# Second buffer for the accumulator tile U2, and a transposed layout of actT, in a macaron encoder block

## The chip, the cores and the metric

The kernel runs on one core of a Trainium2 chip. The metric is the device time of one execution in microseconds (us); lower is better. The core has a matrix engine (PE, with its weight loads shown as PEld), a vector engine (DVE), an activation engine (ACT), a general engine (POOL) and a queue that issues the transfers (SP). The engines run side by side and wait for each other through semaphores; each one takes its own instructions strictly in the order of the program.

## The reference, cut to what matters

One layer on x of shape (1, 1024, 1024) in float32: a half-step FFN, attention with an output projection, and a second half-step FFN. The change touches the two FFNs and everything that reads or writes the transposed activations.

```
def _swiglu(x, w_gate, w_up, w_down):
    return (jax.nn.silu(x @ w_gate) * (x @ w_up)) @ w_down

f = _swiglu(_rmsnorm(x, ffn1_pre_g[l]), ffn1_w_gate[l], ffn1_w_up[l], ffn1_w_down[l])   # D_FF = 2816
x = x + 0.5 * _rmsnorm(f, ffn1_post_g[l])
h = _rmsnorm(x, mix_pre_g[l])
qkv = h @ w_qkv[l]
...                                     # two kinds of attention
x = x + _rmsnorm(heads @ w_out[l], mix_post_g[l])
f = _swiglu(_rmsnorm(x, ffn2_pre_g[l]), ffn2_w_gate[l], ffn2_w_up[l], ffn2_w_down[l])
x = x + 0.5 * _rmsnorm(f, ffn2_post_g[l])
```

## The kernel before

**Precision.** Every float32 operand of a matrix product is split into two parts, HI and LO. A product is three matmuls per 128 rows of contraction: HI by HI, HI by LO, LO by HI (`PASSES`).

**actT** (line 67) holds the normalised activations transposed, contraction on the partitions: 2 parts, 8 token blocks `T` of 128, 8 contraction blocks `k` of 128. It lives through the whole program. `to_actT` (line 110) fills it from PE transposes, with one copy on ACT (line 107) and one subtraction on DVE (line 108) for each four blocks. It is then read by the FFNs, by the q/k/v projection (line 567, one 128x128 block at a time as weights) and, refilled by the attention's `finish` (line 870), by the output projection (line 1002, again as weights). `spare` (line 533) uses a part of it as scratch for sums of squares.

**The FFN's gate and up products.** `D_FF` is cut into 22 blocks of 128 columns. Block 0 is computed plainly (`plain`). Blocks i = 1 to 21 are computed in steps of seven products, a Strassen-like scheme on a 2 x 2 split of the contraction and of the tokens: `ORDER` is P1, P6, P2, P7, P5, P4, P3, and `LAST` (step 21 only) has P7 ahead of P2. Each product is 12 matmuls of 128x128 weights by 128x512 moving values (line 288). The moving operand of P1, P2, P4 and P3 is a slice of actT: four token blocks of one contraction block, so four runs of 128 values that lie eight blocks apart. The moving operand of P6, P7 and P5 is one of three `tx` tiles, also four runs of 128 values, four blocks apart. P1 and P2 accumulate in one PSUM tile `pa`, P6 in `pb`, P7 and P4 in `pc`, P5 and P3 in `pd`.

**The combinations** (`gate_up`, line 395) follow each product on ACT and DVE. After P1, ACT copies `pa` into the SBUF tile U2 (line 409). After P6, DVE adds `pb` into U2 (line 411). After P4, DVE forms C21 (line 423), and after P3 it adds `pd` into U2 (line 426). `glu` (lines 445 and 446) takes SiLU of one half on ACT and multiplies on DVE; P3's `glu` reads U2 last. P2 goes on accumulating in `pa`, so its first matmul may start only when line 409 has read `pa`. U2, C21 and U3 have one buffer each, so line 409 of step i+1 may write U2 only when `glu` of P3 of step i has read it.

**The weights** of each product are combined from raw gate/up blocks on POOL (lines 212 to 225) and split in HI (ACT, line 117) and LO (POOL or DVE, line 118) into a `wgu` buffer. There are five such buffers: a split for the product four places ahead is put into the program before each product (`feed`), and has to wait until an older product has released its buffer.

**Order.** All of this is written out in Python; each engine's order is the order of the calls. On ACT one step goes: split, `glu` of P3 of the step before (line 445), line 409, split, split, `glu` of P2, split, and so on.

Of the kernel before, what the change touches and what calls it, by code (L numbers as in the profile page):

```python
# [10 lines left out]
F32 = mybir.dt.float32  # L11
FR = mybir.dt.float32r
I32 = mybir.dt.int32
AF = mybir.ActivationFunctionType
# [10 lines left out]
NT = S // 128  # L25
# [6 lines left out]
HI, LO = 0, 1  # L32
# [4 lines left out]
def tile_macaron_block(ctx, tc, x, f1_pre, f1_post, f1_g, f1_u, f1_d, mix_pre, mix_post, w_qkv,  # L37
                       qg, kg, w_out, f2_pre, f2_post, f2_g, f2_u, f2_d, rope_a, rope_b, mask, out):
    nc = tc.nc
    PE, ACT, DVE, POOL, SP = nc.tensor, nc.scalar, nc.vector, nc.gpsimd, nc.sync  # L40
# [14 lines left out]
    const = ctx.enter_context(tc.tile_pool(name="const", bufs=1))  # L55
# [8 lines left out]
    POOL.memset(eps, EPS)  # L64
    ACT.activation(stat.tile([128, 1], F32, name="ss"), eps, AF.Sqrt)
    identr = const.tile([128, 128], FR, name="identr")
    actT = const.tile([128, 2, NT, 8, 128], FR, name="actT")
    ident = f32(identr)

    def load_bcast(t, g, scale=None):  # L70
# [5 lines left out]
    MARK = {}  # L76
# [19 lines left out]
    def rms_pair(srcs, junks):  # L96
        ss = stat.tile([128, 2], F32, name="ss2")
        for n in range(2):
            MARK["act"] = ACT.activation(junks[n], srcs[n], AF.Square, accum_out=ss[:, n:n + 1]).ins
        r = rstd(ss, 2, 1.0 / D)  # L100
        return [r[:, n:n + 1] for n in range(2)]

    def turn(src, hv, lv, ps):
        p = ps.tile([128, 4, 128], F32, name="pd")
        for j in range(4):
            PE.transpose(out=p[:, j, :], in_=src[:, 128 * j:128 * j + 128], identity=ident)
        ACT.activation(hv, p, AF.Copy)  # L107
        return DVE.tensor_tensor(lv, p, f32(hv), op=OP.subtract)  # L108

    def to_actT(T, xn, ps):  # L110
        for h in range(2):
            last = turn(xn[:, 512 * h:512 * h + 512], actT[:, HI, T, 4 * h:4 * h + 4, :],
                        actT[:, LO, T, 4 * h:4 * h + 4, :], ps)
        return last

    def split(hi, lo, raw, eng=POOL):
# [3 lines left out]
    class Ffn:  # L120
# [151 lines left out]

        def rhs(self, name, hl, k):
            if name == "B11":
                return actT[:, hl, 0:4, k, :]
            if name == "B21":
                return actT[:, hl, 0:4, 4 + k, :]
            if name == "B22":
                return actT[:, hl, 4:8, 4 + k, :]
            if name in ("B12", "T4"):  # L280
                return actT[:, hl, 4:8, k, :]
            return self.T[int(name[1]) - 1][:, hl, :, k, :]

        def product(self, p, w, name, first, c0=0, c1=4):
# [36 lines left out]
        def turn_combo(self, name, y, ps):  # L321
            n = int(name[1])
            for i in range(4):
                T, d = {1: (i, 0), 2: (i + 4, 1), 3: (i + 4, 0), 4: (i, 1)}[n]
                hv, lv = [actT[:, z, 4 + i, 0:4, :] if n == 4 else self.T[n - 1][:, z, i] for z in (HI, LO)]
                turn(y[:, T, 512 * d:512 * d + 512], hv, lv, ps)

        def keep(self, j):
# [65 lines left out]

        def gate_up(self, i, prod, ps, y, psd):
            def U(name):
                return self.u.tile([128, 4, 128], F32, name=name)

            tt, add, s = DVE.tensor_tensor, OP.add, self.S
            n = (self.ORDER if i < NF - 1 else self.LAST).index(prod)  # L400
            if i == 1 and 0 < n < 5:
                self.turn_combo(("T2", "T3", "T1", "T4")[n - 1], y, psd)
            p = self.bank(i, ps, self.BANK[prod])
            first = prod in ("P1", "P6", "P7", "P5")
            name = {"P1": "B11", "P6": "T2", "P7": "T3", "P5": "T1", "P2": "B21", "P4": "T4", "P3": "B22"}[prod]
            self.product(p, self.W[i, prod], name, first)
            if prod == "P1":
                s["u2"], s["c21"] = U("U2"), U("C21")
                ACT.activation(s["u2"], p, AF.Copy)  # L409
            elif prod == "P6":  # L410
                tt(s["u2"], s["u2"], p, op=add)
            elif prod == "P7":
                s["u3"] = U("U3")
                tt(s["u3"], s["u2"], p, op=add)
            elif prod == "P5":
                s["h1"] = self.new_h(i, 1)
                tt(s["u3"], s["u3"], p, op=add)  # L417
                self.glu(s["h1"][64:128], s["u3"], s["c21"])
            elif prod == "P2":
                s["h0"] = self.new_h(i, 0)  # L420
                self.glu(s["h0"][0:64], p, s["h0"])
            elif prod == "P4":
                tt(s["c21"], s["u2"], p, op=add)
                self.glu(s["h0"][64:128], s["c21"], s["h0"])
            elif prod == "P3":
                tt(s["u2"], s["u2"], p, op=add)
                self.glu(s["h1"][0:64], s["u2"], s["c21"])
            if i == NF - 1 and n == 3:
                self.close_tx(2)
                self.raw.release()  # L430
                self.load_left(self.AHEAD)
                self.open_down()
            if n == 6 and i % 2 == 1 and i < NF - 1:
                self.keep(i // 2)
            if n == 6 and i >= NF - 2:
                for half in range(2):
                    SP.dma_start(self.hd["h", i, half], self.H[i][half])
            if n == 6 and i == NF - 1:
                self.close_tx(1)
                self.u.release()  # L440
                self.us = open_pool("us" + self.tag, side=self.near)
                self.U = self.us.tile([128, 4, 512], F32, name="U")
# [67 lines left out]
    for T in range(NT):  # L510
        if T == 2:
            f1.split_plain()
        xn = y[:, T, :]
# [6 lines left out]
        last = to_actT(T, xn, psd)  # L520
# [10 lines left out]


    def spare(n):
        return actT[:, n % 2, n // 2].rearrange("p k f -> p (k f)")

    def post_norm(Ts, g, res, dst, junk, xr):
        yt = [y[:, T, :] for T in Ts]
# [8 lines left out]
    WQ = {}  # L546
# [15 lines left out]
    def qkv_mm(j, T, ps, bufs=3):  # L562
        p = ps.tile([128, 256], F32, name="pq", bufs=bufs)
        n = 0
        for k in range(8):
            for a, b in PASSES:
                PE.matmul(p, actT[:, a, T, k, :], WQ[j][:, b, k, :], start=(n == 0), stop=(n == 23))  # L567
                n += 1
        return p

# [37 lines left out]
    for t in range(2, NT + L1):  # L608
# [6 lines left out]
        if t in (2, 4):  # L615
            j = t // 2 - 1
# [7 lines left out]
        if 0 <= t - L0 < NT:  # L624
            T = TS[t - L0]
            to_actT(T, y[:, T, :], psd)
        if 0 <= t - L1 < NT:
            T = TS[t - L1]
# [166 lines left out]
    for j in range(2, 9):  # L795
# [6 lines left out]
        if 2 <= j <= 4:  # L802
            ra = tmp.tile([128, NT, 256], F32, name="ra")
            nh = 2 if j == 2 else 4
            ss = tmp.tile([128, NT, nh], F32, name="ssA")
        for T in range(NT):
            p = qkv_mm(j, T, psq)
# [62 lines left out]
    def finish(o, head, Ts, tt=None):  # L870
        b0 = 64 * (head % 2)
        t1, t2 = tt or (at.tile([64, 256], F32, name="ot1"), at.tile([128, 256], F32, name="ot2"))
        ACT.activation(t1, o[64:128, :], AF.Copy)
        ACT.activation(t2[0:64], o[0:64, :], AF.Copy)
        POOL.tensor_tensor(t2[b0:b0 + 64], t2[0:64], t1, op=OP.add)
        tv = t2[b0:b0 + 64].rearrange("p (t f) -> p t f", t=2)
        hv = actT[b0:b0 + 64, HI, Ts, head // 2, :]
        lv = actT[b0:b0 + 64, LO, Ts, head // 2, :]
        POOL.tensor_scalar(hv, tv, 1.0, 1.0, op0=OP.mult, op1=OP.mult)
        POOL.tensor_tensor(lv, tv, f32(hv), op=OP.subtract)  # L880

# [45 lines left out]
    for i in range(N + 3):  # L927
        if i < N:
            head, T, e = UN[i]
# [4 lines left out]
        if 0 <= i - 2 < N:  # L934
            head, T, e = UN[i - 2]
# [3 lines left out]
        if 0 <= i - 3 < N:  # L939
            head, T, e = UN[i - 3]  # L940
# [51 lines left out]
    for t in range(NT + 2):  # L992
        if t < NT:
            T = t
            xr = wo.tile([128, D], F32, name="xr")
            SP.dma_start(xr, x1d[T])
            p = pso.tile([128, 1024], F32, name="pz")
            for dh in range(2):
                n = 0
                for c in range(8):  # L1000
                    for a, b in PASSES:
                        PE.matmul(p[:, 512 * dh:512 * dh + 512], actT[:, a, T, c, :],
                                  WO[c][:, b, 512 * dh:512 * dh + 512], start=(n == 0), stop=(n == 23))
                        n += 1
            z = y[:, T, :]
            r = rms_scale(p, z)
            DVE.scalar_tensor_tensor(z, p, r, g_mo, op0=OP.mult, op1=OP.mult)
            (DVE if T == NT - 1 else POOL).tensor_tensor(z, z, xr, op=OP.add)
            SP.dma_start(x2d[T], z)
        if 0 <= t - 1 < NT:  # L1010
            T = t - 1
            z = y[:, T, :]
            jk = wo.tile([128, D], F32, name="xr")
            r = rms_scale(z, jk)
            DVE.scalar_tensor_tensor(z, z, r, g_pre, op0=OP.mult, op1=OP.mult)
        if 0 <= t - 2 < NT:
            if t == 2:
                f2.split_plain()
            if t == NT + 1:
                f2.plain((psg0, None), 0)  # L1020
            last = to_actT(t - 2, y[:, t - 2, :], pso)
# [19 lines left out]
    for n, T in enumerate(TS):  # L1041
# [4 lines left out]
        if n >= 2:  # L1046
            xr, yt = fin.tile([128, D], F32, name="xr", bufs=6), y[:, T, :]
            SP.dma_start(xr, x2d[T])
            if n == 7:
                ss = stat.tile([128, 3], F32, name="ss3")  # L1050
                jk = psj.tile([128, D], F32, name="junk")
                for c in range(2):
                    ACT.activation(jk[:, 512 * c:512 * c + 512], yt[:, 512 * c:512 * c + 512], AF.Square,
                                   accum_out=ss[:, c:c + 1])
# [82 lines left out]
```

## Time and profile before

| what | value |
|---|---|
| median of 3 runs | 2077.77 us (2077.45 to 2078.15) |
| the profiled execution's own time | 2079.25 us |
| its span, first to last instruction | 2077.5 us (1.75 us lie around it) |
| busy: PE, PEld, DVE, ACT, POOL | 95%, 81%, 64%, 48%, 50% |
| mean granted clock of PE | 0.99 of full speed |

A timeline row gives the start, the time from the first start to the last end of the merged instructions, the engine, the line, the operation, and in brackets the idle time of that engine just before and what ended it. The end of a matmul is modelled and overlaps the next one, so the length of a product is best read from its start to the next product's start. "Waits" rows add up such idle times by who waited for whom. A waiting instruction with several semaphores is put down to the one that came last by the profile, which need not be the one that it needed.

### The profile page before, as it was taken

How to read it: one execution, taken by the hardware profiler on the slowest of the kernel's cores; microseconds unless marked ns; L12 is line 12 of the kernel's file. 1: busy time of each engine (PE TensorE's matmuls, PEld its weight loads, DVE VectorE, ACT ScalarE, POOL GpSimd, SP SyncE). 2: the span in 40 equal slices, each digit the busy share in tenths (PEclk: the TensorE clock that was granted, in tenths of full speed). 3: DMA queues.
4: the chain of work that ended last, by engine and by line, in shares of the span. 5: the costliest groups of instructions: out<-in, count | busy, mean ns of one | idle time of the engine just before them, and what ended most of it. 6: DMA issues, size and time to landing. Idle time of an engine off the chain costs nothing. (4 is left out here: it accounts for less than half of the span.)

```text
span 2077.5 us, 30443 instructions
## 1 busy us (share of the span) xinstructions
PE 1983.2 (95%) x10728; PEld 1676.4 (81%) x10728; DVE 1333.0 (64%) x2255; ACT 1005.9 (48%) x1892; POOL 1048.3 (50%) x894
## 2 busy tenths in 40 slices
PE   7999999999999799999999999999999999999996
PEld 6777777777888699998999998887777777778884
DVE  7545544547668855766999888356545444576688
ACT  5433333334444433436999999234333333344443
POOL 4555656565050614233777887315565655651504
PEclk9999999999999899999999999999999999999998
DMA  4232322326533543233040643222323232365434
GB/s 147 75 98 87 116 92 87 112 87 228 177 117 95 199 130 101 67 102 77 2 138 1 207 137 90 102 77 71 100 78 125 79 101 84 115 221 170 127 97 172
DMA packets 210681, 233.01 MB, mean 112 GB/s; under 512 B 21088, under 2 KB 147040, under 8 KB 210400
## 3 DMA queue, kind: packets, MB, share of 16 engines
q1 hardware_dynamic: 210528, 231.06, 35.3%
q8 instruction: 85, 1.39, 0.3%
q14 instruction: 68, 0.56, 0.1%
HBM read 164.95 MB, written 66.06 MB: 111 GB/s over the span
## 5 line engine op out<-in xcount | busy, mean ns | idle before, releaser
L118 POOL TENSOR_TENSOR wgu<-rawgu,wgu 128x512 fp32r<-128x512 f32 x216 | 306.8, 1428 | 385.4 <-ACT wgu L117 358.8
L117 ACT ACTIVATE wgu<-rawgu 128x512 fp32r<-128x512 f32 x302 | 181.7, 627 | 368.0 <-POOL rawgu L225 190.5
L288 PE MATMUL pa<-actT,wgu 128*128 128x512 f32 (+1 forms) x1080 | 270.4, 398 | 29.7 <-ACT U L409 28.8
L356 PE MATMUL pd<-wgu 128*128 128x512 f32 x1140 | 272.4, 390 | 3.5 <-DVE wgu L118 3.2
L288 PEld LDWEIGHTS pa<-actT,wgu 128*128 128x128 f32 x1080 | 198.6, 190 | 89.2 <-ACT U L409 44.5
L356 PEld LDWEIGHTS pd<-wgu 128*128 128x128 f32 x1140 | 213.0, 188 | 52.5 <-DVE wgu L118 6.7
L567 PE MATMUL pq<-wq,actT 128*128 128x256 f32 x1728 | 217.7, 284 | 0.7 <-ACT actT L107 0.7
L567 PEld LDWEIGHTS pq<-wq,actT 128*128 128x128 f32 x1728 | 208.9, 190 | 1.3 <-ACT actT L107 1.0
L117 ACT ACTIVATE wgu<-b 128x512 fp32r<-128x512 f32 x148 | 93.0, 631 | 204.7 <-PE pd L356 114.8
L118 DVE TENSOR_TENSOR wgu<-b,wgu 128x512 fp32r<-128x512 f32 x144 | 120.3, 837 | 103.8 <-ACT wgu L117 103.4
L767 POOL TENSOR_SCALAR P<-P,il 128x1024 f32<-128x1024 f32 (+1 forms) x128 | 130.6, 1020 | 64.3 <-DVE il L766 61.1
L446 DVE TENSOR_TENSOR h<-h,C 64x512 f32<-64x512 f32 x42 | 51.5, 1226 | 156.9 <-ACT h L445 156.9
L868 DVE TENSOR_TENSOR PT<-pt,PT 128x512 fp32r<-128x512 f32 (+1 forms) x256 | 146.2, 612 | 2.0 <-ACT PT L867 2.0
L288 PE MATMUL pd<-actT,wgu 128*128 128x512 f32 x552 | 136.2, 395 | 0.0
L288 PE MATMUL pc<-actT,wgu 128*128 128x512 f32 x552 | 136.0, 394 | 0.0
L867 ACT ACTIVATE PT<-pt 128x512 fp32r<-128x512 f32 (+1 forms) x256 | 125.4, 544 | 10.5 <-PE pt L864 7.1
L864 PE MATMUL pt<-identr,P 128*128 128x128 f32 x896 | 125.0, 275 | 1.7 <-ACT vst L702 1.1
L288 PEld LDWEIGHTS pd<-actT,wgu 128*128 128x128 f32 x552 | 103.3, 187 | 25.7 <-DVE U L417 0.6
L288 PEld LDWEIGHTS pc<-actT,wgu 128*128 128x128 f32 x552 | 103.3, 187 | 25.0 <-DVE actT L108 0.4
L288 PE MATMUL pb<-tx,wgu 128*128 128x512 f32 x504 | 122.3, 391 | 0.0
L288 PE MATMUL pc<-tx,wgu 128*128 128x512 f32 x504 | 122.3, 391 | 0.0
L288 PE MATMUL pd<-tx,wgu 128*128 128x512 f32 x504 | 121.3, 389 | 0.0
(190 smaller groups left out, 3898.9 us busy)
## 6 DMA issues: line engine op xcount, KB each, us to landing
hd<-h SPq DMA_DIRECT2D x140, 256.0 KB, 2.9
h<-hd SPq DMA_DIRECT2D x140, 256.0 KB, 2.9
rawgu<-in_ffn_w_gate_dram SPq DMA_DIRECT2D x88, 256.0 KB, 3.0
rawgu<-in_ffn_w_up_dram SPq DMA_DIRECT2D x88, 256.0 KB, 3.7
b<-in_ffn_w_down_dram SPq DMA_DIRECT2D x88, 256.0 KB, 3.4
bkT<-kd SPq DMA_DIRECT2D x32, 320.0 KB, 7.3
rawq<-in_w_qkv_dram SPq DMA_DIRECT2D x16, 512.0 KB, 4.7
bV<-vd SPq DMA_DIRECT2D x8, 640.0 KB, 4.4
```

The costliest lines, as they stand in the source:

```text
L117: ACT.activation(hi, raw, AF.Copy)
L118: return eng.tensor_tensor(lo, raw, f32(hi), op=OP.subtract).ins
L288: PE.matmul(p[:, c0:c1, :], w[:, a, k, :], self.rhs(name, b, k)[:, c0:c1, :], start=(first and n == 0), stop=(n == 11), skip_group_check=True)
L356: PE.matmul(p, A[:, a, 128 * i:128 * i + 128], B[:, b, :], start=(first and start and n == 0), stop=(end and n == 2), skip_group_check=True)
L446: DVE.tensor_tensor(dst, s[64:128], c[64:128], op=OP.mult)
L567: PE.matmul(p, actT[:, a, T, k, :], WQ[j][:, b, k, :], start=(n == 0), stop=(n == 23))
L767: POOL.tensor_scalar(P[:, 0:w], P[:, 0:w], il, 1.0, op0=OP.mult, op1=OP.mult)
L864: PE.transpose(out=p[:, j, :], in_=col(P, b0 + j), identity=ident)
L867: ACT.activation(hv, p[:, 0:n, :], AF.Copy)
L868: DVE.tensor_tensor(lv, p[:, 0:n, :], f32(hv), op=OP.subtract)
```

## The change

The tile U2 gets two buffers (C21 and U3 keep one). actT changes from [part, token block, contraction block, 128] to [part, contraction block, token block, 128], and every slice of it follows: four token blocks of one contraction block now lie side by side, so the moving operand of P1, P2, P4 and P3 is one run of 512 values. The weights of lines 567 and 1002 are one run of 128 values as before. What writes four contraction blocks of one token block (`to_actT`, and one `turn_combo`) now writes four runs of 128 values that lie eight blocks apart, where it wrote one run of 512. Nothing is added or taken out, and every engine's instructions stand in the same order as before. The added line shifts line numbers by one from line 100 on.

```
-    actT = const.tile([128, 2, NT, 8, 128], FR, name="actT")
+    actT = const.tile([128, 2, 8, NT, 128], FR, name="actT")
...
+            src = srcs[n] if len(junks[n].shape) == 2 else srcs[n].rearrange("p (k f) -> p k f", k=8)
...
-            last = turn(xn[:, 512 * h:512 * h + 512], actT[:, HI, T, 4 * h:4 * h + 4, :],
-                        actT[:, LO, T, 4 * h:4 * h + 4, :], ps)
+            last = turn(xn[:, 512 * h:512 * h + 512], actT[:, HI, 4 * h:4 * h + 4, T, :],
+                        actT[:, LO, 4 * h:4 * h + 4, T, :], ps)
...
             if name == "B11":
-                return actT[:, hl, 0:4, k, :]
+                return actT[:, hl, k, 0:4, :]
...                                                    (B21, B22, B12 and T4 alike)
-                hv, lv = [actT[:, z, 4 + i, 0:4, :] if n == 4 else self.T[n - 1][:, z, i] for z in (HI, LO)]
+                hv, lv = [actT[:, z, 0:4, 4 + i, :] if n == 4 else self.T[n - 1][:, z, i] for z in (HI, LO)]
...
-                return self.u.tile([128, 4, 128], F32, name=name)
+                return self.u.tile([128, 4, 128], F32, name=name, bufs=2 if name == "U2" else 1)
...
-        return actT[:, n % 2, n // 2].rearrange("p k f -> p (k f)")
+        return actT[:, n % 2, :, n // 2]
...
-                PE.matmul(p, actT[:, a, T, k, :], WQ[j][:, b, k, :], start=(n == 0), stop=(n == 23))
+                PE.matmul(p, actT[:, a, k, T, :], WQ[j][:, b, k, :], start=(n == 0), stop=(n == 23))
...
-        hv = actT[b0:b0 + 64, HI, Ts, head // 2, :]
+        hv = actT[b0:b0 + 64, HI, head // 2, Ts, :]
```

ACT in the program of before, from `glu` of P3 of step 7 (C21 from the U2 of step 7, U2_1607) over line 409 of step 8 (U2_1753) to `glu` of P2 of step 8. The names in brackets are the semaphores that an instruction waits for, here those that DVE, PE and ACT raise and one of a transfer:

```order
L445 ACTIVATE C21_1608<-U2_1607 64x512 [waits DVE_49,Activation_49]
L409 ACTIVATE U2_1753<-pa_1740 128x512 [waits DVE_49,PE_49]
L117 ACTIVATE wgu_1759<-rawgu_1610 128x2x4x64
L117 ACTIVATE wgu_1778<-rawgu_1610 128x2x4x64 [waits PE_49]
L445 ACTIVATE h_1795<-pa_1740 64x512 [waits DMAHW4_49,PE_49]
```

The same place in the changed program:

```order
L446 ACTIVATE C21_1608<-U2_1607 64x512 [waits DVE_49,Activation_49]
L410 ACTIVATE U2_1753<-pa_1740 128x512 [waits PE_49]
L118 ACTIVATE wgu_1759<-rawgu_1610 128x2x4x64
L118 ACTIVATE wgu_1778<-rawgu_1610 128x2x4x64 [waits PE_49]
L446 ACTIVATE h_1795<-pa_1740 64x512 [waits DMAHW4_49,PE_49]
```

No instruction moved. The copy into U2 (line 409, now 410) no longer waits for DVE; it waits for PE alone, which is the end of P1.

## Rows read from the trace of the kernel before

**Rows 1.** The page's first part: busy us (share of span) and instructions of each engine.
```profile
PE 1983.2 (95%) x10728; PEld 1676.4 (81%) x10728; DVE 1333.0 (64%) x2255; ACT 1005.9 (48%) x1892; POOL 1048.3 (50%) x894
```

**Rows 2.** Waits of PE, 95 to 465 and 1450 to 1820 us: total, times, longest.
```profile
PE pa L288 <- ACT U L409: 12.7, 18, 1.0
...
PE pa L288 <- ACT U L409: 12.3, 18, 0.7
```

**Rows 3.** Timeline of PE over one step, P2 of step 8 to P2 of step 9.
```profile
207.04 3.06 PE L288 MATMUL pa<-actT,wgu 128*128 128x512 f32 x12 [0.69 <-ACT U L409]
209.94 2.90 PE L288 MATMUL pc<-tx,wgu 128*128 128x512 f32 x12
212.68 2.88 PE L288 MATMUL pd<-tx,wgu 128*128 128x512 f32 x12
215.40 2.95 PE L288 MATMUL pc<-actT,wgu 128*128 128x512 f32 x12
...
221.00 2.96 PE L288 MATMUL pa<-actT,wgu 128*128 128x512 f32 x12
223.79 2.90 PE L288 MATMUL pb<-tx,wgu 128*128 128x512 f32 x12
227.38 3.06 PE L288 MATMUL pa<-actT,wgu 128*128 128x512 f32 x12 [0.69 <-ACT U L409]
```

**Rows 4.** Timeline of ACT over the same step.
```profile
210.14 0.59 ACT L445 ACTIVATE h<-pa 64x512 f32<-64x512 f32 x1 [2.11 <-PE pa L288]
210.76 0.63 ACT L117 ACTIVATE wgu<-rawgu 128x512 fp32r<-128x512 f32 x1
215.42 1.15 ACT L117 ACTIVATE wgu<-rawgu 128x512 fp32r<-128x512 f32 x2 [4.03 <-POOL rawgu L214]
...
221.91 0.63 ACT L117 ACTIVATE wgu<-rawgu 128x512 fp32r<-128x512 f32 x1 [4.69 <-POOL rawgu L225]
222.57 0.63 ACT L445 ACTIVATE h<-C 64x512 f32<-64x512 f32 x1
...
225.28 0.63 ACT L445 ACTIVATE C<-U 64x512 f32<-64x512 f32 x1 [1.42 <-DVE U L426]
226.73 0.60 ACT L409 ACTIVATE U<-pa 128x512 f32<-128x512 f32 x1 [0.81 <-PE pb L288]
```

**Rows 5.** Timeline of POOL over the same step.
```profile
211.47 1.29 POOL L118 TENSOR_TENSOR wgu<-rawgu,wgu 128x512 fp32r<-128x512 f32 x1 [2.56 <-ACT wgu L117]
...
214.09 1.29 POOL L214 TENSOR_TENSOR rawgu<-rawgu 128x512 f32<-128x512 f32 x1
216.13 3.01 POOL L118 TENSOR_TENSOR wgu<-rawgu,wgu 128x512 fp32r<-128x512 f32 x2 [0.74 <-ACT wgu L117]
...
220.59 1.29 POOL L225 TENSOR_TENSOR rawgu<-rawgu 128x512 f32<-128x512 f32 x1
```

**Rows 6.** Timeline of DVE near the end of the same step.
```profile
223.24 1.23 DVE L446 TENSOR_TENSOR h<-h,C 64x512 f32<-64x512 f32 x1 [4.15 <-ACT h L445]
224.50 0.69 DVE L426 TENSOR_TENSOR U<-U,pd 128x512 f32<-128x512 f32 x1
...
225.95 0.69 DVE L446 TENSOR_TENSOR h<-C,U 64x512 f32<-64x512 f32 x1 [0.16 <-ACT C L445]
```

**Rows 7.** Matmuls by line and shape: count, busy us, mean ns of one, idle before.
```profile
L567 PE MATMUL pq<-wq,actT 128*128 128x256 f32 x1728 | 217.7, 284 | 0.7 <-ACT actT L107 0.7
...
L288 PE MATMUL pc<-actT,wgu 128*128 128x512 f32 x552 | 136.0, 394 | 0.0
...
L288 PE MATMUL pc<-tx,wgu 128*128 128x512 f32 x504 | 122.3, 391 | 0.0
...
L1002 PE MATMUL pz<-wo,actT 128*128 128x512 f32 x384 | 90.3, 394 | 0.5 <-DVE wo L118 0.5
...
L899 PE MATMUL po<-PT,bV 128*128 128x256 f32 x320 | 46.4, 290 | 0.5 <-ACT PT L867 0.3 <-DVE PT L868 0.2
...
L846 PE MATMUL sp<-bkT,bqT 128*128 128x512 f32 x128 | 44.5, 429 | 0.0
```

More of the change, by code (lines that the diff above doesn't have):

```diff
@@ L98, in rms_pair @@
         for n in range(2):
-            MARK["act"] = ACT.activation(junks[n], srcs[n], AF.Square, accum_out=ss[:, n:n + 1]).ins
+            src = srcs[n] if len(junks[n].shape) == 2 else srcs[n].rearrange("p (k f) -> p k f", k=8)
+            MARK["act"] = ACT.activation(junks[n], src, AF.Square, accum_out=ss[:, n:n + 1]).ins
         r = rstd(ss, 2, 1.0 / D)
@@ L274, in rhs @@
             if name == "B11":
-                return actT[:, hl, 0:4, k, :]
+                return actT[:, hl, k, 0:4, :]
             if name == "B21":
-                return actT[:, hl, 0:4, 4 + k, :]
+                return actT[:, hl, 4 + k, 0:4, :]
             if name == "B22":
-                return actT[:, hl, 4:8, 4 + k, :]
+                return actT[:, hl, 4 + k, 4:8, :]
             if name in ("B12", "T4"):
-                return actT[:, hl, 4:8, k, :]
+                return actT[:, hl, k, 4:8, :]
             return self.T[int(name[1]) - 1][:, hl, :, k, :]
@@ L876, in finish @@
         tv = t2[b0:b0 + 64].rearrange("p (t f) -> p t f", t=2)
-        hv = actT[b0:b0 + 64, HI, Ts, head // 2, :]
-        lv = actT[b0:b0 + 64, LO, Ts, head // 2, :]
+        hv = actT[b0:b0 + 64, HI, head // 2, Ts, :]
+        lv = actT[b0:b0 + 64, LO, head // 2, Ts, :]
         POOL.tensor_scalar(hv, tv, 1.0, 1.0, op0=OP.mult, op1=OP.mult)
@@ L1001, in tile_macaron_block @@
                     for a, b in PASSES:
-                        PE.matmul(p[:, 512 * dh:512 * dh + 512], actT[:, a, T, c, :],
+                        PE.matmul(p[:, 512 * dh:512 * dh + 512], actT[:, a, c, T, :],
                                   WO[c][:, b, 512 * dh:512 * dh + 512], start=(n == 0), stop=(n == 23))
```

## The prediction

> **What bounds the kernel now.** The page's first part comes first: PE is busy 95% of the span [rows 1], so only two things can move the time much, a stall of PE or the length of its matmuls. The view of waits says where PE still stalls. Inside the gate/up loops of the two FFNs one wait is left, P2's first matmul for the copy into U2 at line 409: 18 times in each FFN, 25.0 us together [rows 2]. So the next view is the timeline of one such step.
>
> P2 of step 8 starts at 207.04 and P2 of step 9 at 227.38: a cycle is 20.34 us long [rows 3]. How long would PE alone need? P7 to P6 start at 209.94 and 223.79, which is 13.85. P6 would take what P5 takes, 215.40 - 212.68 = 2.72, and an unhindered P2 what P1 takes, 223.79 - 221.00 = 2.79 (P2 now takes 209.94 - 207.04 = 2.90: after a stall its first weight load is exposed). That gives 19.36 us. PE loses 0.98 us per cycle, more than the 0.69 shown as idle, because the exposed load and the tail of the modelled matmul hide a part.
>
> What holds line 409? Its row says that its idle time of 0.81 was ended by PE's pb [rows 4], which is P6. But line 409 reads pa and writes U2; P6 touches neither. What does touch U2 is DVE's multiplication of P3's `glu`, from 225.95 to 226.64 [rows 6], and line 409 starts at 226.73. The profile names P6 because P6 ends at about the same moment. The place where the wait stands in the program, shown above, agrees: DVE and PE before, PE alone after.
>
> **The chain behind it.** The same rows show that line 409 is the last link of a chain that starts at the end of P2 one step earlier. ACT's SiLU of P2 (210.14, it waited for pa) and the split behind it (210.76) [rows 4]; seven POOL instructions, from 211.47 to 221.88, with ACT's split of 215.42 between them, which itself waited for POOL [rows 4, 5]; ACT's split at 221.91 (it waited for POOL) and the SiLU of P4 at 222.57 [rows 4]; DVE's multiplication at 223.24 and the addition of P3 at 224.50 [rows 6]; ACT's SiLU of P3 at 225.28; DVE's multiplication at 225.95; line 409 at 226.73; P2 at 227.38, 0.05 after line 409 ends [rows 3, 4, 6]. Every link starts when the one before it ends. So the loop has two periods, 19.36 for PE alone and 20.34 for this chain, and the longer one counts.
>
> **Part 1, the second buffer of U2.** It takes one link out: line 409 need not wait for the multiplication. ACT then goes from the SiLU of 225.28 straight to line 409. Neighbours on ACT start 222.57 - 221.91 = 0.66 apart [rows 4], so line 409 starts at 225.94 in place of 226.73: **0.79 us earlier**. P1 has long ended by then. P2 starts at 226.59, and the cycle is 20.34 - 0.79 = 19.55 us. That is still 0.19 more than PE alone needs, so the chain keeps the pace, and the whole 0.79 is gained, but no more. The multiplication itself stays on DVE, where its result goes to the next step's stores; nobody on the chain waits for it any more. The sum: 36 cycles x 0.79 = **28.4 us**. Step 2 (no stall in it) and step 21 (P7 stands ahead of P2) gain nothing, nor does step 1, whose copy has no earlier U2 to wait for. Were the chain to fall away wholly, the gain would be 36 x 0.98 = 35.3 us: the bound on one side. The bound on the other side is nothing (a rival, below).
>
> What is triggered by the earlier copy: ACT's two splits behind it come 0.79 earlier and POOL's LO part with them, which then waits longer for the split at 210.76. Their buffers are released by P1 and P6, no later than now. No DMA and no queue changes its place.
>
> **Part 2, the layout of actT.** No row shows a 512-value run of actT as moving operand, so I bound it. P1 reads four runs out of actT in 2.79 us, P5 four runs out of tx in 2.72 [rows 3]; by shape 394 against 391 ns a matmul [rows 7]. So actT costs 0.07 us a product more than another tile of the same shape. The nearest row for the new form is line 1002: 512 values in one run, actT as the other operand, 394 ns [rows 7], no better than now. I take **nothing** for it. The far end is 0.07 for each product that PE paces. In the chain-bound cycles that is P2 alone, since the chain starts at P2's end: 36. P1, P4 and P3 lie beside POOL's work there, and what they save becomes a longer stall. Outside them about 40 products read actT: in each FFN 8 of block 0, 4 of step 1, 2 of step 2, 2 of step 20 and 4 of step 21. So 76 x 0.07 = 5.3 us gain at most; the other end is dearer reading, below.
>
> First the row, then a rule: P1 and P5 have the same shape and run length and differ by 0.07 us [rows 3]. The Trainium skill (SBUF — State Buffer, Specifications) says that a read is at full rate while it uses whole 16-byte lines; a run of 128 four-byte values does so in either layout, and by that part 2 gives nothing, as I took it. The same page (Who interferes with whom) says that PE never waits on anyone; the 0.07 between P1 and P5, which that sentence doesn't explain, speaks against taking it as settled.
>
> The writes: line 117's split writes runs of 64 values in 0.63 us, line 409 one run of 512 in 0.60 [rows 4]. So the evictions into actT, now runs of 128, cost at most 0.03 us each: 56 on ACT, 1.7 us were all of them on the path; most lie under PE's work, and I take 0. The weight reads of lines 567 and 1002 keep their runs of 128; I take 0. Should a matmul of line 567 move to the 290 ns of line 899, the costliest of the same shape, 1728 x 6 ns = 10 us would be lost [rows 7]; a gain of half the 3 ns between the L288 forms would give 2.6.
>
> **The rivals.**
> (a) The layout pays: contiguous reading costs what tx costs. For it: tx shows that actT's 0.07 isn't in the shape. Against: line 1002. Gain 28.4 + 5.3 = 33.7.
> (b) The chain shortens further, because the earlier POOL and DVE work collides less (DVE's multiplication of 223.24 took 1.23, that of 225.95 0.69 [rows 6]), and PE paces the loop: 35.3, and with the layout's 0.07 in all 144 products of those cycles and 40 others, up to 48. Against: these collisions hang on the same chain and move with it.
> (c) The buffer saves nothing because line 409 really waits for P6, as the profile names it. For: that row. Against: P6 doesn't write what line 409 reads. Time as before, within 1 us.
> (d) Slower: one run of 512 is dearer for PE, as line 846 reads its keys, 429 ns against 394 [rows 7]. 48 matmuls a cycle x 35 ns = 1.68; PE alone then needs 21.04, the chain is hidden, and the time grows by 36 x 0.70 + 40 x 0.42 = 42 us. It decides from some 16 ns a matmul on, where 36 x (48 x 0.016 - 0.98) + 40 x 12 x 0.016 is about 0. Against: line 1002 has one run too, at 394.
> (e) A weaker gain: another link takes over, or line 567 goes the way of line 899: 10 to 24 us gained.
>
> **How the numbers follow.** The profiled execution took 2079.25 us, 1.5 above the median; by its own time the sum is 2079.25 - 28.4 = 2050.9, and against the median 2077.77 it is **2049.4**, which I forecast at 45%. (a) gives 2044.1 at 33%, (b) 2030 to 2042.5 at 8%, (e) 2054 to 2068 at 7%, (c) 2078 at 3%, (d) 2120 at 4%. The range 2041 to 2054 holds the forecast with its small costs, (a), and the upper edges of (b) and (e), and leaves out some 17%. A measurement of this kernel can tell about 0.2%, 4.2 us, from no change: faster 0.93, same 0.03, slower 0.04.
>
> **What would show it.** In the changed profile the wait of P2 for the copy into U2 stays, some 36 times, but shrinks to 0.2 us or less in idle; the copy starts 0.66 after the SiLU of P3; the cycle from P2 to P2 is 19.5 to 19.6. P1, P4 and P3 at 2.79 say that the layout does nothing, at 2.72 that (a) holds, and then the stall of P2 should have grown by 0.2. Cycles of 19.36 or less would be (b), of 20.3 (c). I would be wrong above all if POOL's part of the chain changed its length, since that is more than half of it.

## The result and the profile after

The changed kernel takes 2055.1 us (2053.84 to 2057.43, four runs) where the kernel before takes 2077.96 (2077.45 to 2078.87): a ratio of 0.9894, 95% interval 0.9882 to 0.9906. (The ratios here are estimates over the runs of a series; they can differ by some 0.0005 from the quotient of the two medians.) The forecast was 2049, its range ended at 2054. The sign and the place were right, the gain was 22.9 us in place of 28.4. The profiled execution took 2054.44 us, its span is 2052.7.

In the rows of the changed kernel line 410 is the copy into U2 that was line 409. First the page's first part of the changed kernel, the row that answers to [rows 1]:

```profile
PE 1978.4 (96%) x10728; PEld 1675.0 (82%) x10728; DVE 1338.1 (65%) x2255; ACT 1005.4 (49%) x1892; POOL 1056.0 (51%) x894
```

Then the waits of PE in the two gate/up loops (total, times, longest), 95 to 465 and 1435 to 1805 us, which answer to [rows 2]:

```profile
PE pa L289 <- ACT U L410: 2.5, 8, 0.3
...
PE pa L289 <- ACT U L410: 2.4, 8, 0.3
```

The wait fell from 25.0 us to 4.9. But it is listed 8 times in each FFN where it was listed 18 times: every other cycle has it, and in the others the view lists no idle time. The forecast had it some 36 times, at 0.2 us or less. The timeline of PE over two cycles, from P2 of step 8 to P2 of step 10, shows the same (it answers to [rows 3]):

```profile
201.86 3.05 PE L289 MATMUL pa<-actT,wgu 128*128 128x512 f32 x12
...
215.82 2.96 PE L289 MATMUL pa<-actT,wgu 128*128 128x512 f32 x12
218.62 2.90 PE L289 MATMUL pb<-tx,wgu 128*128 128x512 f32 x12
221.82 3.05 PE L289 MATMUL pa<-actT,wgu 128*128 128x512 f32 x12 [0.30 <-ACT U L410]
...
241.34 0.96 PE L289 MATMUL pa<-actT,wgu 128*128 128x512 f32 x3
```

The first cycle is 221.82 - 201.86 = 19.96 us, the second 241.34 - 221.82 = 19.52 (the last row is cut off by the window, its start is not). Before, the cycles were 20.32 to 20.37 almost throughout. Over the whole trace 16 of the 36 cycles are about 19.97 us and 20 about 19.52. P1 takes 218.62 - 215.82 = 2.80, as before (2.79 in [rows 3]).

From P2 of step 2 to P2 of step 20 the two loops took 366.13 and 366.32 us before, together 732.45, and take 354.85 and 355.10 now, together 709.95: 22.5 us gained, where the medians differ by 22.9. Had all 36 cycles become 19.52, it would have been 732.45 - 36 x 19.52 = 29.7 us. So the question is what makes 16 cycles some 0.45 us too long.

ACT over the start of the longer cycle, which answers to [rows 4], shows the predicted step in place:

```profile
200.55 0.63 ACT L446 ACTIVATE C<-U 64x512 f32<-64x512 f32 x1 [1.42 <-DVE U L427]
201.21 0.60 ACT L410 ACTIVATE U<-pa 128x512 f32<-128x512 f32 x1
...
205.56 0.63 ACT L118 ACTIVATE wgu<-rawgu 128x512 fp32r<-128x512 f32 x1
210.65 1.15 ACT L118 ACTIVATE wgu<-rawgu 128x512 fp32r<-128x512 f32 x2 [4.46 <-POOL rawgu L215]
```

The copy starts 0.66 after the SiLU of P3, as forecast, where it started 226.73 - 225.28 = 1.45 after it [rows 4]. P2 starts at 201.86, 0.05 after the copy's end at 201.81, though no idle time is listed for it: the chain still ends in P2. But the split of line 118 waits 4.46 us for POOL, which was 4.03 [rows 4]. POOL in the same place, and one cycle later (it answers to [rows 5]):

```profile
206.27 1.74 POOL L119 TENSOR_TENSOR wgu<-rawgu,wgu 128x512 fp32r<-128x512 f32 x1 [2.49 <-DMA rawgu<-in_ffn_w_up_dram]
207.97 1.29 POOL L214 TENSOR_TENSOR rawgu<-rawgu 128x512 f32<-128x512 f32 x1
...
211.36 3.00 POOL L119 TENSOR_TENSOR wgu<-rawgu,wgu 128x512 fp32r<-128x512 f32 x2 [0.74 <-ACT wgu L118]
...
226.22 1.29 POOL L119 TENSOR_TENSOR wgu<-rawgu,wgu 128x512 fp32r<-128x512 f32 x1 [2.57 <-ACT wgu L118]
```

The first POOL instruction of the chain, the split after P2, takes 1.74 us in the longer cycles and 1.29 in the shorter ones: 0.45, which is the difference of the cycles. What runs beside it? DVE at that time:

```profile
201.21 0.69 DVE L447 TENSOR_TENSOR h<-C,U 64x512 f32<-64x512 f32 x1 [0.16 <-ACT C L446]
201.94 3.12 DVE L338 TENSOR_TENSOR h<-h 128x512 f32<-128x512 f32 x3
204.97 0.68 DVE L412 TENSOR_TENSOR U<-U,pb 128x512 f32<-128x512 f32 x1
205.57 0.69 DVE L119 TENSOR_TENSOR wgu<-rawgu,wgu 128x512 fp32r<-128x512 f32 x1
206.17 0.69 DVE L338 TENSOR_TENSOR h<-h 128x512 f32<-128x512 f32 x1
```

These are additions of which neither the front part nor the prediction spoke. After every odd step `keep` stores the finished h tiles and queues four sums of them (one addition and three subtractions, called late additions here; line 337 before, 338 now). `add_late` puts them between the next products, and each has a store of its own on SP. On DVE three of them stand right behind the multiplication of P3's `glu`, the fourth behind a split. The fourth runs from 206.17 to 206.86, and POOL's split starts at 206.27, inside it. In the kernel before, the same four stood like this (DVE, P2 of step 8 starts at 207.04):

```profile
205.61 0.69 DVE L446 TENSOR_TENSOR h<-C,U 64x512 f32<-64x512 f32 x1 [0.16 <-ACT C L445]
206.34 3.13 DVE L337 TENSOR_TENSOR h<-h 128x512 f32<-128x512 f32 x3
209.38 0.68 DVE L411 TENSOR_TENSOR U<-U,pb 128x512 f32<-128x512 f32 x1
209.98 0.68 DVE L118 TENSOR_TENSOR wgu<-rawgu,wgu 128x512 fp32r<-128x512 f32 x1
210.58 0.68 DVE L337 TENSOR_TENSOR h<-h 128x512 f32<-128x512 f32 x1
```

The fourth ended at 211.26, and POOL's split started at 211.47 [rows 5], 0.21 later. The run of DVE instructions hangs on the multiplication, and the multiplication hangs on the SiLU of P3; neither moved against the other. P2, and with its end POOL's split, moved 0.8 us towards them: the three additions began 0.70 ahead of P2 before and begin 0.08 behind it now. So POOL's split landed inside the fourth.

### The profile page after: what moved, and what is told of

Read it like the earlier page. It is cut to its first block, busy times and chain, and to the rows that moved or that the text cites. A ratio compares the mean times of both kernels' runs of the same rounds, so it can differ in the third digit from the quotient of the medians.

```text
span 2052.7 us, 30441 instructions
## 1 busy us (share of the span) xinstructions
PE 1978.4 (96%) x10728; PEld 1675.0 (82%) x10728; DVE 1338.1 (65%) x2255; ACT 1005.4 (49%) x1892; POOL 1056.0 (51%) x894
## 5 line engine op out<-in xcount | busy, mean ns | idle before, releaser
L119 POOL TENSOR_TENSOR wgu<-rawgu,wgu 128x512 fp32r<-128x512 f32 x216 | 315.5, 1469 | 354.2 <-ACT wgu L118 332.2
```

The source lines that it names most:

```text
L119: return eng.tensor_tensor(lo, raw, f32(hi), op=OP.subtract).ins
```

## The experiments

**Theory 1**: the fourth late addition on DVE, running beside POOL's split, makes that split 0.45 us longer in every other cycle; this and nothing else makes every other cycle long. **Theory 2**: the transfers of those steps do it (stores of the sums, or the loads of raw weights behind them on SP's queue; the profile's row of the long split names such a load as what ended POOL's wait). And it was open whether the layout had any part in the gain.

### The two parts alone

The second buffer in the kernel before, in the old layout:

```
+                return self.u.tile([128, 4, 128], F32, name=name, bufs=2 if name == "U2" else 1)
```

> The kernel before with the second buffer of U2 alone; actT keeps its old layout. If the layout gives nothing (as predicted), this is the whole change: 2055 us, within 2 us of the changed kernel, and the cycles from P2 to P2 alternate between 19.5 and 20.0 us as in the changed kernel. If the layout costs or gives something that the buffer hides, the time differs from the changed kernel's by what it costs: up to 5 us either way.

Measured: 2055.98 us (2055.37 to 2056.69), ratio 0.989 (0.9876 to 0.9905), the cycles 19.5 and 20.0 in turn, as in the changed kernel. The other half is the changed kernel with one buffer for every accumulator tile:

```
-                return self.u.tile([128, 4, 128], F32, name=name, bufs=2 if name == "U2" else 1)
+                return self.u.tile([128, 4, 128], F32, name=name)
```

> The changed kernel with one buffer for U2: the layout of actT alone. If the layout gives nothing: 2078 us, every cycle 20.33 us, P1 2.79 us long as before. If contiguous reading pays where PE paces (some 40 products outside the loop's cycles, and P2 in 36 of them): up to 5 us less, 2073. If it costs: above 2080.

Measured: 2077.04 us beside 2078.72 of the kernel before, ratio 0.9997 (0.9987 to 1.0006). Its waits of PE, 90 to 455 us, read as [rows 2] do:

```profile
PE pa L289 <- ACT U L410: 13.1, 18, 1.3
```

So the buffer is the whole change, both its gain and its every-other-cycle loss, and the layout gives nothing that can be measured.

### The additions left out, after and before

```
-            s2, s3, s4 = [self.dn.tile([128, 512], F32, name="h") for _ in range(3)]
+            s2 = s3 = s4 = a21
...
-                def made(k=k, o=o, p=p, q=q, op=op):
-                    DVE.tensor_tensor(o, p, q, op=op)
-                    SP.dma_start(self.hd[k, j], o)
+                def made(k=k, p=p):
+                    SP.dma_start(self.hd[k, j], p)
```

> The changed kernel without the four late additions on VectorE (the sums of the kept tiles, line 338); the stores stay and write unsummed tiles, so this part of the computation is left out. Theory 1 (the fourth late addition runs beside GpSimd's split of line 119 and makes it 1.74 us in place of 1.29 in every other cycle): the split is 1.29 in all cycles, every cycle is 19.5 us, and some 17 x 0.44 = 7.5 us are gained: 2047 to 2048. Theory 2 (the transfers of those steps, stores of the kept tiles or loads of raw weights, slow GpSimd): the long cycles stay at 19.96, 2055 us.

Measured: 2049.06 us, ratio 0.9854 (0.984 to 0.9869). POOL in the two cycles that follow each other, first the one that was long:

```profile
207.03 1.29 POOL L119 TENSOR_TENSOR wgu<-rawgu,wgu 128x512 fp32r<-128x512 f32 x1 [2.57 <-ACT wgu L118]
...
226.56 1.29 POOL L119 TENSOR_TENSOR wgu<-rawgu,wgu 128x512 fp32r<-128x512 f32 x1 [2.56 <-ACT wgu L118]
```

The long split is gone, the cycles are 19.4 to 19.6 (one of 19.88), and the wait of P2 for the copy, 90 to 455 us, is listed once with 0.2 us. The same edit in the kernel before:

> The kernel before (one buffer for U2, old layout) without the four late additions on VectorE; their stores stay and write unsummed tiles, so this part of the computation is left out. Theory 1 (the collision exists only because P2 now starts earlier while the additions stay where they were): before the change the additions ended ahead of GpSimd's split and cost nothing, so every cycle stays at 20.33 us and the time at 2078, within 2 us. If the additions cost something in the old kernel too, for example by holding the chain in itself: up to 8 us less, and then they are no effect of the change.

Measured: 2078.43 us beside 2078.59, ratio 0.9996 (0.9987 to 1.0005). PE in this kernel, which is one line shorter, so that the copy is line 408; P2 of two steps:

```profile
205.57 3.06 PE L288 MATMUL pa<-actT,wgu 128*128 128x512 f32 x12 [0.69 <-ACT U L408]
...
225.91 3.06 PE L288 MATMUL pa<-actT,wgu 128*128 128x512 f32 x12 [0.69 <-ACT U L408]
```

The cycle is 225.91 - 205.57 = 20.34, that of [rows 3]. So the same additions cost nothing that can be measured before the change and some 6 to 7 us after it (2049.06 against 2055.1, and against the 2055.98 of the second buffer alone, in the same series). It was not settled yet which half of an addition did it, since without the sum its store need not wait either.

### The additions kept, the waits of their stores taken away

```
-                def made(k=k, o=o, p=p, q=q, op=op):
+                def made(k=k, o=o, p=p, q=q, op=op, t={5: a22, 2: a11, 3: a22, 6: a12}[k]):
                     DVE.tensor_tensor(o, p, q, op=op)
-                    SP.dma_start(self.hd[k, j], o)
+                    SP.dma_start(self.hd[k, j], t)
```

> The changed kernel with its four late additions in place on VectorE, but each store writes a tile that is not summed, so that no store waits for an addition (the sums are computed and not kept: the results of this part are left out). It keeps VectorE's side of the additions and takes the wait of the transfer queue away. Theory 1 (VectorE's addition beside GpSimd's split lengthens the chain): as the changed kernel, 2055 us, cycles alternating between 19.5 and 20.0, the split after P2 1.74 us long. Theory 2 (stores that wait for the additions hold back the loads of raw weights behind them in the queue, and GpSimd waits for those): all cycles 19.5, 2049 us.

Measured: 2056.38 us, ratio 0.9901 (0.9884 to 0.9917). DVE and then POOL in a long cycle:

```profile
207.94 0.68 DVE L338 TENSOR_TENSOR h<-h 128x512 f32<-128x512 f32 x1
```

```profile
208.05 1.74 POOL L119 TENSOR_TENSOR wgu<-rawgu,wgu 128x512 fp32r<-128x512 f32 x1 [2.50 <-ACT wgu L118]
```

No store waits for a sum any more, POOL's wait is now put down to ACT alone, and the split is still 1.74 us long behind the start of the addition. Theory 2 falls for the changed kernel; theory 1 stands.

### The additions moved

One addition less ahead of P2, so that the last one comes later:

```
-                self.add_late(1)
+                if it[0] != "G" or it[2] not in ("P2",):
+                    self.add_late(1)
```

> The changed kernel, nothing left out, with one late addition moved: none is put ahead of P2 any more, so that the fourth one comes later, ahead of P7 or P5. Theory 1 (a late addition of VectorE beside GpSimd's split is what lengthens every other cycle): the split of line 119 after P2 is back at 1.29 us, unless the multiplication of line 447 now takes the place of the addition beside it; where it is, the cycles are 19.5 throughout and 2047 to 2048 us are reached. Theory 2 (transfers): 2055 us, the long cycles stay.

Measured: 2057.68 us, ratio 0.9897 (0.9882 to 0.9912): the 2047 to 2048 us of theory 1 are not reached. The cycles are 19.5 to 19.6 and 20.0 in turn, as without the move. DVE, then POOL:

```profile
206.69 1.23 DVE L338 TENSOR_TENSOR h<-h 128x512 f32<-128x512 f32 x1
```

```profile
206.08 1.29 POOL L119 TENSOR_TENSOR wgu<-rawgu,wgu 128x512 fp32r<-128x512 f32 x1 [2.49 <-DMA rawgu<-in_ffn_w_up_dram]
207.33 1.74 POOL L214 TENSOR_TENSOR rawgu<-rawgu 128x512 f32<-128x512 f32 x1
```

The split was there first: it takes its 1.29, and the addition waits for it and takes 1.23 in place of 0.69. Its end, at 207.92, then lies 0.59 us behind the start of line 214, the next POOL instruction of the chain, which takes the 0.45 us. The collision was moved by one place and cost the same. The split's row names a load here too, and it is 1.29 us long: the name says nothing of its length.

Two additions moved in among POOL's work:

```
-                self.add_late(1)
+                if it[0] != "G" or it[2] in ("P1", "P6"):
+                    self.add_late(1)
```

> The changed kernel, nothing left out: two late additions behind the multiplication of P3 as before, the other two moved behind the multiplication of P5, where GpSimd runs the two splits and an addition that the chain consists of. Theory 1: two collisions in every other cycle in place of one; the cycle of those steps is 19.53 + 2 x 0.44 = 20.4 us, against 19.97 with one, and the time 2055 + 17 x 0.44 = 2062 us; at least one of the pair must show, so not under 2054. Theory 2 (only the place beside P2's split matters, because that split is late there): all cycles 19.53, 2049 us.

Measured: 2064.53 us, ratio 0.9931 (0.9917 to 0.9944); 18 of the 36 cycles are long, 15 of them 20.18 to 20.25 (the others 20.09, 20.14 and 20.34). DVE, then POOL:

```profile
215.51 3.37 DVE L338 TENSOR_TENSOR h<-h 128x512 f32<-128x512 f32 x2
```

```profile
216.71 1.62 POOL L224 TENSOR_TENSOR rawgu<-rawgu 128x512 f32<-128x512 f32 x1
218.41 1.62 POOL L226 TENSOR_TENSOR rawgu<-rawgu 128x512 f32<-128x512 f32 x1
```

The pair of additions ends at 215.51 + 3.37 = 218.88, and line 226 has started 0.47 before that; line 224 started as far inside the first of the pair. Two POOL instructions of the chain are longer now, each by 0.33 where 0.44 was expected, together 0.66, and the cycle is 20.18 - 19.53 = 0.65 longer. With 18 such cycles that is 11.7 us above the kernel without additions, 2060.8; the rest of the 2064.5 is not accounted for (1.6 us of it lie in the second FFN's step before the loop).

Two additions in each step, behind the multiplication of P3 (`self.last`), so that they end well ahead of the split:

```
...
-                self.add_late(1)
+                if it[0] != "G":
+                    self.add_late(1)
+                elif it[2] == "P1" and self.late:
+                    with tc.issue_after(self.last):
+                        self.add_late(2)
```

> The changed kernel, nothing left out: two late additions behind the multiplication of P3 in each step, in place of three and one in every other step. They end some 1.3 us ahead of GpSimd's split after P2. Theory 1: no instruction of GpSimd on the chain takes 1.74 us any more, all cycles are 19.52 to 19.57, and the time is that of the kernel without the additions, 2049 us. Theory 2 (the mere number of additions, stores or buffers costs, not their place): 2055 us.

Measured: 2058.44 us, ratio 0.9907 (0.9893 to 0.9921): not what either theory gave its number for. The long cycles are 19.9 to 20.6 in the profiled execution, which took 2062.06, the longest of the four. POOL after P2 of a long cycle (P2 starts at 204.46, the next at 224.42, a cycle of 19.96):

```profile
208.87 1.29 POOL L119 TENSOR_TENSOR wgu<-rawgu,wgu 128x512 fp32r<-128x512 f32 x1 [2.49 <-ACT wgu L118]
210.58 1.29 POOL L214 TENSOR_TENSOR rawgu<-rawgu 128x512 f32<-128x512 f32 x1 [0.41 <-issue]
```

The collision is gone as forecast (1.29), but POOL stands still for 0.41 us before line 214. That line reads a raw weight block, so the next view is SP's queue (start, length, line, transfer):

```profile
203.72 0.37 SPq L181 DMA_DIRECT2D rawgu<-in_ffn_w_gate_dram  x1
204.53 0.34 SPq L334 DMA_DIRECT2D hd<-h  x1
205.25 2.02 SPq L339 DMA_DIRECT2D hd<-h  x2
207.33 0.43 SPq L181 DMA_DIRECT2D rawgu<-in_ffn_w_up_dram  x1
```

The load of the up block stands behind two stores that wait for the additions, and is issued at 207.33. The loads of this line take 3.3 us to land (median of the trace), so by that it would land at about 210.6, when line 214 starts. The trace's view of line 181 counts 10 waits of POOL's line 214 for its loads, 6.2 us together. Theory 2's mechanism is real, in this kernel. The same kernel with the two stores put behind the loads:

```
...
-                    SP.dma_start(self.hd[k, j], o)
+                    self.stores.append(lambda: SP.dma_start(self.hd[k, j], o))
...
+                if it[0] != "G" or it[2] == "P7":
+                    while self.stores:
+                        self.stores.pop(0)()
```

> The kernel with two late additions a step, nothing left out, with their two stores put into the queue ahead of P7, behind the loads of raw weights of the step, where they stood between them. If the gap of 0.4 us that GpSimd showed ahead of line 214 in every other step came from a load of raw weights behind a store that waited for an addition, the gap goes, all cycles are 19.5 and the time is 2049 us. If it came from something else, 2058 us as measured without the move.

Measured: 2048.72 us (2047.7 to 2048.91), ratio 0.9865 (0.9851 to 0.988). SP's queue, then POOL:

```profile
202.22 0.34 SPq L334 DMA_DIRECT2D hd<-h  x1
202.61 0.43 SPq L181 DMA_DIRECT2D rawgu<-in_ffn_w_up_dram  x1
203.13 1.85 SPq L339 DMA_DIRECT2D hd<-h  x2
```

```profile
206.56 1.29 POOL L119 TENSOR_TENSOR wgu<-rawgu,wgu 128x512 fp32r<-128x512 f32 x1 [2.49 <-DMA rawgu<-in_ffn_w_up_dram]
207.81 1.29 POOL L214 TENSOR_TENSOR rawgu<-rawgu 128x512 f32<-128x512 f32 x1
```

The load is issued 0.39 us after the store of line 334, where it was 2.80 after it (207.33 - 204.53). The gap is gone, and the cycles are 19.4 to 19.6 (one of 19.82). With the whole computation in place the kernel reaches the time that the prediction had forecast for the change.

### The chain taken off P2, in both layouts

ACT's copy put ahead of the SiLU of P3 of the step before, so that it waits for P1 alone; two late additions a step, ahead of P6 (`end_step` does P3's `glu` and the `keep` of the step before):

```
             if prod == "P1":
-                s["u2"], s["c21"] = U("U2"), U("C21")
-                ACT.activation(s["u2"], p, AF.Copy)
+                s["u2"] = U("U2")
+                with tc.issue_after(ACT.activation(s["u2"], p, AF.Copy).ins):
+                    self.end_step(i - 1)
+                s["c21"] = U("C21")
...
```

> The changed kernel, nothing left out: ScalarE's copy into U2 stands ahead of the SiLU of P3 of the step before (in the changed kernel behind it), so that it waits for P1 alone and the chain no longer ends in P2; two late additions in each step. If the chain was all that held P2, TensorE paces the loop: cycles of 19.36 to 19.40 us, no wait of P2 for the copy, 2078 - 36 x 0.98 = 2043 us, 5 to 6 below the kernel without late additions. If something else holds P2 or GpSimd's part closes another ring (a split that arrives late for P6 or P2), cycles stay at 19.5 and the time at 2048 to 2050, and the profile names the split in place of the copy.

Measured: 2044.57 us (2043.62 to 2046.49), ratio 0.9837 (0.9824 to 0.9851), the best of this study. ACT (line 455 is the SiLU of `glu` here), then PE:

```profile
218.40 0.60 ACT L410 ACTIVATE U<-pa 128x512 f32<-128x512 f32 x1
219.68 0.63 ACT L455 ACTIVATE C<-U 64x512 f32<-64x512 f32 x1 [0.68 <-DVE U L429]
```

```profile
201.56 2.96 PE L289 MATMUL pa<-actT,wgu 128*128 128x512 f32 x12
...
215.40 2.96 PE L289 MATMUL pa<-actT,wgu 128*128 128x512 f32 x12
218.20 2.90 PE L289 MATMUL pb<-tx,wgu 128*128 128x512 f32 x12
220.94 2.95 PE L289 MATMUL pa<-actT,wgu 128*128 128x512 f32 x12
```

The cycle is 220.94 - 201.56 = 19.38 us, and the view of PE's waits lists none from 90 to 455 us. The prediction had worked out 19.36 for PE alone. Here every product is paced by PE, so this loop would show the price of the layout. The same kernel in the old layout:

> The kernel with the copy ahead of the SiLU and two late additions a step, in the old layout of actT, nothing left out. TensorE paces this loop with no wait for the copy, so here every product that reads actT would show its price in the time. If the layout gives nothing: 2045 us, P1 2.80 us long as in the new layout. If contiguous reading pays 0.07 us a product, as rival (a) had it: 4 products x 36 cycles x 0.07 = 10 us more than the new layout, 2055.

Measured: 2045.58 us (2042.27 to 2046.16), ratio 0.9848 (0.9833 to 0.9863), whose interval holds 0.9837. P1 and P6 in its timeline of PE:

```profile
215.17 2.96 PE L288 MATMUL pa<-actT,wgu 128*128 128x512 f32 x12
217.97 2.90 PE L288 MATMUL pb<-tx,wgu 128*128 128x512 f32 x12
```

P1 takes 217.97 - 215.17 = 2.80, as in the new layout. From P2 of step 2 to P2 of step 20 the two loops take 348.72 and 349.20 us, in both layouts. The 10 us of rival (a) are not there.

## Why the prediction was wrong, and where it was right

**What bounds the kernel: right.** The one wait named was the one that went, PE alone was put at 19.36 us a cycle and the kernel that reaches it runs at 19.37 to 19.40.

**Which semaphore the copy waits for: right.** Line 409's wait was put down to PE's pb by the profile, and the prediction held DVE's multiplication to be the cause. With the second buffer the copy starts 0.66 after the SiLU; rival (c) is out.

**The size of the link: right.** 0.79 us a cycle were forecast; the undisturbed cycles are 19.52 on average where those before were 20.35, some 0.82 less. Over 36 cycles this is 29.7 - 28.4 = 1.3 us more than the sum had; where the 0.03 a cycle comes from was not followed.

**The layout: right**, and shown three ways: alone it gives a ratio of 0.9997, without it the gain is the same, and in the loop that PE paces both layouts give P1 2.80 us and the same length of the loops. Rivals (a) and (d) are out.

**The step that failed** is the reason against rival (b): "these collisions hang on the same chain and move with it". It held for another collision of the chain, that of P5's multiplication on DVE with the second of two splits on POOL: the two splits take 3.01 us before ([rows 5], with the multiplication from 217.26 to 217.97) and 3.00 after (from 211.36, with the multiplication from 212.50 to 213.22). It doesn't hold for two branches that leave the chain at different links. The link that the change takes out lies between the SiLU of P3 and P2; DVE's multiplication and what is queued behind it leave the chain ahead of that link, POOL's split leaves it behind P2, and so one moved by 0.8 us against the other. Of the multiplication the prediction said that nobody on the chain waits for it any more, but not what DVE does next. Its list of what the earlier copy triggers named ACT's splits and POOL's LO part, but no work of DVE; the late additions were in the same trace, 0.21 us clear of the split. The error is one term: 16 cycles x 0.45 = 7.2 us that were put at nothing. The undisturbed 29.7 less 7.2 make the 22.5 by which the loops differ; that is the same cycles added up another way, and the independent measure of the term is the kernel without the additions, which is 6 to 7 us faster. The link's extra 1.3 us hid a part: the forecast was missed by 28.4 - 22.9 = 5.5 us, not by 7.

The prediction's last sentence, that it would be wrong above all if POOL's part of the chain changed its length, named the place, and rival (e), a gain of 10 to 24 us, held the outcome with a chance of 7%. It was priced as another link that takes over; in fact the same chain got longer. The range cut (e) off at its upper edge, and missed by 1.1 us. A chain whose POOL and DVE parts were already seen to run into each other (1.23 against 0.69 in [rows 6]) should have had the price of one more such collision as a bound: 18 cycles (the additions come in every other step) x 0.54 us, a time of up to 2059. POOL's side had a price as well, in the row of [rows 5] that the prediction read only as a part of the chain: two splits take 3.01 us where one takes 1.29, so 3.01 - 2 x 1.29 = 0.43 too long. By these two rows the chain holds about 1 us of collisions in every cycle, as much as PE loses to it; that taking those out alone would let PE set the pace is an estimate, and no run tried it.

What stays open: the 0.03 us a cycle above, the 3.7 us of the kernel with two collisions that its cycles do not explain, and the spread of the kernel before. The runs of the kernel before reached from 2074.5 to 2082.1 us over the later series, and no run here told why. Differences of 1 to 2 us between kernels are not read for that reason; the lengths of cycles, which agree between the traces of these kernels (19.4 to 19.6 us where the chain sets the pace and nothing new collides), carry the argument.

## What to carry to other kernels

When a change takes a link out of a chain that paces a loop, list what leaves the chain ahead of that link and what leaves it behind: the two groups move against each other by the link's length, and an overlap that was missed by 0.2 us before may be hit after. Then price the hit by a collision that the trace already shows, and look for it on every engine of the two groups, work that is off the critical path included. And when such work is moved, move its stores with an eye to what stands behind them in the transfer queue.

## What the runs showed of the hardware

**DVE and POOL get in each other's way, and either can be the one that pays.** A DVE addition of 0.69 us that was there first made POOL's instruction of the same 128x512 float32 values 1.74 us in place of 1.29; where POOL was there first, DVE took 1.23 to 1.24 us in place of 0.69 (line 446 in [rows 6]). Counted over the changed kernel's trace from 130 to 455 us: 34 POOL instructions started inside a DVE instruction with both operands in SBUF, and all 34 were longer than 1.34 us; 25 started inside a DVE instruction with an operand in PSUM and 92 inside none, and none of these was. The Trainium skill (SBUF — State Buffer, Who interferes with whom) says that a DVE instruction with two SBUF inputs contends with a GpSimd instruction that reads SBUF, and that issue order decides who blocks; the trace agrees in both.

**The price goes by the overlap.** POOL's split that started 0.59 us before the addition's end lost 0.45, and so did line 214 with the same 0.59; line 226 with an overlap of 0.47 lost 0.33. From 130 to 455 us the trace of the changed kernel has eight splits with an overlap of 0.23 that lost 0.09, and that of the kernel before eight with 0.17 that lost 0.03: each time the loss is the overlap less some 0.14 us.

**One store that waits holds the queue behind it.** A load of raw weights was issued 2.80 us behind the store of line 334 with two waiting stores between them, and 0.39 behind it without; 0.41 us of these 2.4 reached POOL, and by it P2.

**The difference of 0.06 to 0.07 us between products that read actT and those that read tx isn't the layout.** P1 takes 2.80 us with four runs of 128 and with one run of 512, P6 2.74 where nothing holds the loop (220.94 - 218.20). Where the difference comes from no run here shows.
